# S5 recurrence of context and latents as one run of 80 states on VectorE

## The chip, the cores and the metric

The kernel runs on one core of a Trainium2 chip. The metric is the device time of one execution in microseconds (us). The engines are TensorE (PE in the profile), VectorE (DVE), ScalarE (ACT), GpSimd (POOL) and SyncE (SP, which here only starts DMAs). Each runs its own instructions in the order in which the program lists them for it, and waits on semaphores for the others.

## The reference, cut to what matters

One inference step through two trunk layers on 640 tokens: 128 of a context (a prompt) and 512 latents. Each layer projects the normed tokens to four mixers that run beside each other (a bidirectional state space model, SSD; a bidirectional S5; differential attention; windowed attention), gates and sums them, and ends with an MLP. The change is in S5, a linear recurrence with complex, diagonal coefficients over tokens, forward and backward, for 32 groups of 16 channels with 64 states each:

```python
def s5_direction(u, lam_re, lam_im, log_step, b_re, b_im, c_re, c_im, s0_re, s0_im):
    step = jnp.exp(log_step.astype(f32))[:, None]
    mag = jnp.exp(lam_re * step)
    ab_re = mag * jnp.cos(lam_im * step)
    ab_im = mag * jnp.sin(lam_im * step)
...
    x_re = (coef_re * bu_re - coef_im * bu_im).at[:, 0].add(ab_re * s0_re - ab_im * s0_im)
    x_im = (coef_re * bu_im + coef_im * bu_re).at[:, 0].add(ab_re * s0_im + ab_im * s0_re)
...
    _, _, s_re, s_im = lax.associative_scan(combine, (a_re, a_im, x_re, x_im), axis=1)
    y = (jnp.einsum('blgn,gmn->blgm', s_re, c_re.astype(f32))
         - jnp.einsum('blgn,gmn->blgm', s_im, c_im.astype(f32)))
    return y, s_re[:, -1], s_im[:, -1]
```

The context starts from zero and its last state is an output. The latents start from a state that is an input (`state_s5`). Everything is float32.

## The kernel before

**Layout.** Tokens lie along the free dimension, features on the 128 partitions. Weights come by DMA as 128x512 tiles (`wr`); ScalarE casts each to a high part (`wh`, L214), and `sub_lo` (L198) subtracts to a low part (`wl`), on VectorE or, for every third tile, on GpSimd. A product is then three matmuls (L225, L226, L227), mostly with 320 columns. TensorE therefore waits for VectorE whenever a `wl` of VectorE comes late.

**The S5 branch.** It takes eight tokens per step, so 640 tokens are 80 steps: 16 of the context and 64 of the latents. Partitions 0 to 63 carry the forward direction and 64 to 127 the backward one. A state column of the tile `st` holds 64 numbers per partition: real and imaginary part of 32 groups. (In the trace `st` and the tile with the inputs and powers are both called `B`.)

- `s5_in` (L725 to L756) multiplies the inputs by a matrix, four groups at a time (L745, into `mx`), and ScalarE copies the increments into `st` with three copies per round (L750 to L752, eight rounds). Column 0 is set to zero, columns 1 to 16 are the context's increments; column 17 is the latents' opening state, copied by GpSimd (L755), and 18 to 81 are the latents' increments.
- `s5_scan` (L758 to L793) turns increments into states. One step `advance` (L760) adds the product of a state and a power of the coefficient to the next: two multiplications into a tile `sc` (L764, L765) and two additions into `st` (L767). The 80 steps are cut into ten blocks of eight. In seven levels all blocks advance by one step at once; then eight single steps, one behind the other, carry the last state of a block over to the next block's (64 elements each); then seven more levels add to the inner columns of each block its opening state times powers 1 to 7. The blocks are shared out: of the eight latent blocks VectorE has two and three (`SCAN = 5`, L54, as two separate parts of 128 and 192 elements), and GpSimd three (192 elements); GpSimd also has the two of the context (`ctx="p"`, L49).
- `s5_out` (L795 to L822) brings the states into the order of the groups with three ScalarE copies per round (`sn`, L807 to L809, eight rounds) and TensorE multiplies them by the output matrices (L814 to L816, into `pb`), 81 columns each.

**Order of the work.** The branches are generators, and the strings of `PLAN` (L58) say which generator makes its next step (`i` for s5_in, `s` for s5_scan, `o` for s5_out, `p` for the projection of the differential attention, `a` for its core, `x` for the projection of the SSD branch, `c` for its core, `g` for the gates, `v` for the window attention's keys). A scheduler then fixes the order of each engine's instructions by a simulated timeline, so an edit in one branch also reorders the others. What runs beside the scan in both layers: the norms and rotary factors of the attention's queries and keys (`qk_finish`, L1168: `qn` L1179, `qks` L1187, `qkn` and `qn` L1172 and L1190 on GpSimd), which TensorE transposes (L1204) and ScalarE evacuates (L1205); the scores and softmax of `diff_core` (`dm` L1426, `dp` L1449, transposes L1455); the convolution of the SSD branch, `cv` (L907, L911, L917: seven operations on 128x646 per tile, on VectorE), which TensorE transposes too; and the projections, with their `wh` and `wl`.

## Time and profile before

| | us |
|---|---|
| median of 3 runs | 3042.03 |
| lowest and highest run | 3039.22, 3045.7 |
| profiled execution, its own time | 3031.18 |
| its span in the trace | 3029.4 |

TensorE is busy 2841.5 us of the span, VectorE 1724.3, ScalarE 1180.8, GpSimd 970.2. The mean clock granted to TensorE is 0.972 of full speed. The first layer's scan begins 234 us after the span's start, the second layer's at 1701 us. In the rows further down, a time stamp counts from the start of the span. Each row of a timeline has the start, the duration, the engine, the line of the code, the operation, the tiles (output, then inputs) with their sizes, and in brackets how long the engine was idle before it and what it then waited for. Consecutive instructions of VectorE overlap in the records by some 0.07 us; where an engine goes on without a pause the distance from one start to the next is what an instruction takes of it.

### The profile page before, as it was taken

What the parts mean: (1) busy time and instruction counts of PE and PEld (TensorE: products, weight loads), DVE (VectorE), ACT (ScalarE), POOL (GpSimd) and SP (SyncE); (2) the same over time, 40 slices, a digit from 0 to 9 for tenths busy, and PEclk for the clock granted to TensorE, in tenths of its full rate; (3) what the DMA queues carried; (4) which work ended last, traced back from release to release, by engine and by line L of the source; (5) the groups of instructions that cost most, each with busy time, mean ns of one, the idle gap of its engine ahead of it and who ended that gap; (6) DMA issues with size and microseconds to landing.
All of it is one profiled execution on the core that took longest, in us unless ns stands there. A gap on an engine that the chain in (4) does not pass through costs nothing.

```text
span 3029.4 us, 54102 instructions
## 1 busy us (share of the span) xinstructions
PE 2841.5 (94%) x20782; PEld 2663.8 (88%) x20782; DVE 1724.3 (57%) x3730; ACT 1180.8 (39%) x2660; POOL 970.2 (32%) x1057
## 2 busy tenths in 40 slices
PE   7888898999899999999999889999999999999999
PEld 5888788898689888899998879888898999999999
DVE  7859847765643456646235686475666436433333
ACT  4343463343344242323234536523535434322322
POOL 3737506523212222424111670264131122211111
PEclk9989999999899999999999999999999999999999
DMA  6752253224432735434444323431252323222222
GB/s 238 239 180 90 71 152 111 81 90 134 145 109 72 239 102 174 146 115 154 153 146 132 121 82 111 140 107 58 91 181 86 110 87 112 63 77 74 74 77 84
DMA packets 241858, 364.21 MB, mean 120 GB/s; under 512 B 42272, under 2 KB 104480, under 8 KB 241600
## 3 DMA queue, kind: packets, MB, share of 16 engines
q1 hardware_dynamic: 226848, 336.97, 35.5%
q10 hardware_dynamic: 14752, 23.78, 2.1%
q8 instruction: 164, 2.69, 0.4%
q14 instruction: 94, 0.77, 0.1%
HBM read 294.98 MB, written 65.68 MB: 119 GB/s over the span
## 4 chain that ended last, share of the span: by engine, by line
PE 71%; DVE 15%; issue 4%; DMA 3%; ACT 3%; POOL 2%; SPq 0%; ACTq 0%; DVEq 0%; POOLq 0%
PE dn L225 20%; PE dn L226 19%; PE dn L227 19%; DVE wl L198 2%; DVE B L767 2%; PE mx L290 1%; PE mx L1287 1%; PE pb L1331 1%; PE mx L1461 1%; PE mx L1325 1%; PE mx L1416 1%; DMA sseg<-acum 1%; DVE sc L764 1%; DVE sc L765 1%; PE mx L745 1%
## 5 line engine op out<-in xcount | busy, mean ns | idle before, releaser
L198 POOL TENSOR_TENSOR wl<-wr,wh 128x512 fp32r<-128x512 f32 x207 | 282.6, 1366 | 1271.2 <-ACT wh L214 1151.3
L214 ACT CAST wh<-wr 128x512 fp32r<-128x512 f32 (+1 forms) x614 | 377.4, 620 | 612.9 <-PE dn L226 539.6
L198 DVE TENSOR_TENSOR wl<-wr,wh 128x512 fp32r<-128x512 f32 (+1 forms) x407 | 325.7, 804 | 304.7 <-ACT wh L214 297.3
L225 PE MATMUL dn<-hh,wh 128*128 128x320 f32 x1328 | 422.6, 319 | 8.4 <-ACT us L697 2.7
L227 PE MATMUL dn<-hh,wl 128*128 128x320 f32 x1328 | 420.2, 317 | 3.4 <-DVE wl L198 3.4
L226 PE MATMUL dn<-hl,wh 128*128 128x320 f32 x1328 | 420.1, 316 | 2.8 <-DVE hl L403 1.5
L225 PE MATMUL dn<-nh,wh 128*128 128x320 f32 x992 | 311.7, 315 | 6.6 <-DVE r L1755 6.6
L225 PE MATMUL dn<-fh,wh 128*128 128x320 f32 x1008 | 313.6, 311 | 2.0 <-DVE s5u L595 1.3
L226 PE MATMUL dn<-nl,wh 128*128 128x320 f32 x992 | 308.9, 312 | 3.9 <-DVE nl L403 1.6
L227 PE MATMUL dn<-fh,wl 128*128 128x320 f32 x1008 | 312.0, 310 | 0.0
L226 PE MATMUL dn<-fl,wh 128*128 128x320 f32 x1008 | 311.8, 309 | 0.0
L227 PE MATMUL dn<-nh,wl 128*128 128x320 f32 x992 | 308.0, 311 | 0.0
L226 PE MATMUL dn<-wl,hh 128*128 128x256 f32 (+1 forms) x880 | 258.2, 294 | 16.3 <-DVE wl L198 14.2
L225 PEld LDWEIGHTS dn<-hh,wh 128*128 128x128 f32 x1328 | 254.3, 192 | 16.5 <-issue 3.1
L225 PE MATMUL dn<-wh,hh 128*128 128x256 f32 (+1 forms) x880 | 259.7, 297 | 8.5 <-DVE dtraw L1216 4.2
L227 PEld LDWEIGHTS dn<-hh,wl 128*128 128x128 f32 x1328 | 254.2, 191 | 8.9 <-DVE wl L198 4.6
L226 PEld LDWEIGHTS dn<-hl,wh 128*128 128x128 f32 x1328 | 254.2, 191 | 7.1 <-POOL hl L198 2.1
L227 PE MATMUL dn<-wh,hl 128*128 128x256 f32 (+1 forms) x880 | 257.1, 293 | 0.0
L1547 DVE SCALAR_TENSOR_TENSOR x<-dn,mod,x 128x192 f32<-128x192 f32 (+2 forms) x240 | 98.0, 437 | 225.2 <-PE dn L227 222.2
L225 PE MATMUL dn<-B,wh 128*128 128x320 f32 x640 | 207.8, 326 | 15.1 <-ACT B L834 4.4
L226 PE MATMUL dn<-B,wh 128*128 128x320 f32 x640 | 203.4, 318 | 0.0
L227 PE MATMUL dn<-B,wl 128*128 128x320 f32 x640 | 201.3, 315 | 0.0
(400 smaller groups left out, 6715.0 us busy)
## 6 DMA issues: line engine op xcount, KB each, us to landing
wr<-in_w_fc_dram SPq DMA_DIRECT2D x256, 256.0 KB, 2.8
wa<-in_w_mod_dram SPq DMA_DIRECT2D x160, 256.0 KB, 4.5
wr<-in_w_gate_dram SPq DMA_DIRECT2D x128, 256.0 KB, 2.8
wr<-in_w_tok_dram SPq DMA_DIRECT2D x80, 256.0 KB, 2.9
wr<-in_w_branch_dram SPq DMA_DIRECT2D x64, 256.0 KB, 3.0
acc<-gth SPq DMA_DIRECT2D x48, 320.0 KB, 3.0
gold<-acc SPq DMA_DIRECT2D x48, 320.0 KB, 3.3
gate<-gah ACTq DMA_DIRECT2D x70, 160.0 KB, 2.0
```

The costliest lines, as they stand in the source:

```text
L198: engine.tensor_tensor(out=out, in0=full, in1=hi, op=ALU.subtract)
L214: nc.scalar.copy(out=hi, in_=raw)
L225: nc.tensor.matmul(ps, sh, vh, start=first, stop=False)
L226: nc.tensor.matmul(ps, sh, vl, start=False, stop=False)
L227: nc.tensor.matmul(ps, sl, vh, start=False, stop=last)
L290: nc.tensor.matmul(acc[r0:r0 + 32, i * 256:i * 256 + 256], cpad[:, k, :], raw(part, k // 2)[:, c0:c0 + 256], start=(n_ < 4), stop=(n_ >= 4),)
L745: nc.tensor.matmul(xs[:, ri, g * NI:(g + 1) * NI], pm[:, ri, g * 128:(g + 1) * 128], U[:, g0 + g], start=True, stop=True)
L764: ve.tensor_tensor(out=pair[:, 0], in0=src, in1=re.to_broadcast(shp), op=ALU.mult)
L765: ve.tensor_tensor(out=pair[:, 1], in0=src[:, :, ::-1], in1=im.to_broadcast(shp), op=ALU.mult)
L767: ve.tensor_tensor(out=dst, in0=dst, in1=pair[:, i], op=ALU.add)
L1287: nc.tensor.matmul(sc[:, n, c0:c0 + (k1 - k0) * 128], qT[rows[n], g, ct], kT[rows[n], k0:k1].rearrange("p k c -> p (k c)"), start=True, st ...
L1547: nc.vector.scalar_tensor_tensor(out=xs, in0=ps[:, c0:c1], scalar=mods[l][:, part * 8 + f, s:s + 1], in1=xs, op0=ALU.mult, op1=ALU.add)
```

## The change

The 16 context steps and the 64 latent steps become one run of 80 columns behind a zero column (`st` columns 0 to 80, no separate opening column), and all of it goes to VectorE.

- `s5_in` copies forward increments of context and latents apart, so that a round has four copies in place of three (the copy of 64x648 elements becomes one of 64x128 and one of 64x512); `s5_out` likewise. GpSimd's copy of the opening state (L755) goes.
- Seven levels: each does two multiplications of 128x640 and two additions, for all ten blocks at once (28 instructions in a layer).
- In place of single steps and inner levels: for each block from the second on, its opening state, broadcast, times powers 1 to 8 at once, so that all eight columns of the block come out together, two multiplications and two additions of 128x512 (nine blocks, 36 instructions). The block's last column is the next one's opening state, so the nine blocks follow one another.
- After the first of these, column 16 is the context's final state. VectorE copies it out (128x64, `s5fin`) for the output's DMA and writes the latents' opening state over it.
- Before there were, in a layer, 144 such instructions on VectorE (56 of 128 elements, 56 of 192 and 32 of 64) and 116 on GpSimd (56 of 192, 28 of 128, 32 of 64). The number of steps of the generator stays 15, and `PLAN` is unchanged.

```diff
--- before.py
+++ after.py
@@ -48,10 +48,8 @@
 
 ENG = dict(
     sub0="v", sub1="p", mf="p", ef="v", xd="p", xw="p", xD="p", off="p", z="v", qkn="p", qka="p", qkc="v",
-    merge="p", diff="v", ctx="p", mn="v",
+    merge="p", diff="v", mn="v",
 )
-
-SCAN = 5
 
 LOW = 3
 WM = 14
@@ -747,50 +745,42 @@
                     )
             xv = xs[:, :, :4 * NI].rearrange("p r (g i) -> p r g i", i=NI)
             sv = st.rearrange("p j r g -> p r g j")[:, :, g0:g0 + 4]
-            nc.scalar.copy(out=sv[0:64, :, :, 1:82], in_=xv[0:64])
+
+            nc.scalar.copy(out=sv[0:64, :, :, 1:17], in_=xv[0:64, :, :, 0:16])
+            nc.scalar.copy(out=sv[0:64, :, :, 17:81], in_=xv[0:64, :, :, 17:81])
             nc.scalar.copy(out=sv[64:128, :, :, 16:0:-1], in_=xv[64:128, :, :, 0:16])
-            nc.scalar.copy(out=sv[64:128, :, :, 81:17:-1], in_=xv[64:128, :, :, 17:81])
+            nc.scalar.copy(out=sv[64:128, :, :, 80:16:-1], in_=xv[64:128, :, :, 17:81])
             if b < 7:
                 yield
-        nc.gpsimd.tensor_copy(out=st[:, 17], in_=s0)
-        var["U"], var["st"], var["pw"] = U, st, pw
-
-    def s5_scan(l, st, pw):
-
-        def advance(ve, dst, src, re, im, n):
+        var["U"], var["st"], var["pw"], var["s0"] = U, st, pw, s0
+
+    def s5_scan(l, st, pw, s0):
+
+        nb = (NI - 1) // 8
+
+        def advance(dst, src, re, im, n):
 
             shp = (128, n, 2, 32)
-            pair = tw([128, 2, n, 2, 32], "sc")
-            ve.tensor_tensor(out=pair[:, 0], in0=src, in1=re.to_broadcast(shp), op=ALU.mult)
-            ve.tensor_tensor(out=pair[:, 1], in0=src[:, :, ::-1], in1=im.to_broadcast(shp), op=ALU.mult)
-            for i in range(2):
-                ve.tensor_tensor(out=dst, in0=dst, in1=pair[:, i], op=ALU.add)
-
-        def power(k):
-            return pw[:, k - 1, 0].unsqueeze(1).unsqueeze(1), pw[:, k - 1, 1:3].unsqueeze(1)
-
-
-        parts = [(nc.vector, 17, SCAN // 2), (nc.vector, 17 + SCAN // 2 * 8, SCAN - SCAN // 2)]
-        parts += [(nc.gpsimd, 17 + SCAN * 8, 8 - SCAN)] * (SCAN < 8) + [(eng("ctx"), 0, 2)]
+            for v, x in ((src, re), (src[:, :, ::-1], im)):
+                t = tw([128, n, 2, 32], "sc")
+                nc.vector.tensor_tensor(out=t, in0=v.to_broadcast(shp), in1=x.to_broadcast(shp), op=ALU.mult)
+                nc.vector.tensor_tensor(out=dst, in0=dst, in1=t, op=ALU.add)
+
         for k in range(1, 8):
-            for ve, j, n in parts:
-                e = j + 8 * n
-                advance(ve, st[:, j + 1 + k:e + 1:8], st[:, j + k:e:8], *power(1), n)
+            advance(
+                st[:, 1 + k:8 * nb + 1:8], st[:, k:8 * nb:8], pw[:, 0:1, 0:1], pw[:, 0:1, 1:3], nb
+            )
             yield
-        for b in range(8):
-            j = 17 + 8 * b
-            advance(nc.vector, st[:, j + 8:j + 9], st[:, j:j + 1], *power(8), 1)
-        advance(eng("ctx"), st[:, 16:17], st[:, 8:9], *power(8), 1)
-        yield
-        for k in range(1, 8):
-            for ve, j, n in parts:
-                e = j + 8 * n
-                if j == 0:
-                    advance(ve, st[:, 8 + k:9 + k], st[:, 8:9], *power(k), 1)
-                else:
-                    advance(ve, st[:, j + k:e:8], st[:, j:e:8], *power(k), n)
-            yield
-        sp.dma_start(out=o["state_s5"][l], in_=st[:, 16])
+        for b in range(1, nb):
+            advance(st[:, 8 * b + 1:8 * b + 9], st[:, 8 * b:8 * b + 1], pw[:, :, 0:1], pw[:, :, 1:3], 8)
+            if b == 1:
+
+                fin = tmp([128, 2, 32], "s5fin", bufs=1)
+                nc.vector.tensor_copy(out=fin, in_=st[:, 16])
+                nc.vector.tensor_copy(out=st[:, 16], in_=s0)
+                sp.dma_start(out=o["state_s5"][l], in_=fin)
+            else:
+                yield
 
     def s5_out(l, U, st, y_d):
 
@@ -804,9 +794,10 @@
             sp.dma_start(out=qm, in_=q_d[b])
             sn = tw([128, 2, 4, NI], "sn")
             sv = st.rearrange("p j r g -> p r g j")[:, :, g0:g0 + 4]
-            nc.scalar.copy(out=sn[0:64], in_=sv[0:64, :, :, 0:81])
+            nc.scalar.copy(out=sn[0:64, :, :, 0:17], in_=sv[0:64, :, :, 0:17])
+            nc.scalar.copy(out=sn[0:64, :, :, 17:81], in_=sv[0:64, :, :, 16:80])
             nc.scalar.copy(out=sn[64:128, :, :, 0:16], in_=sv[64:128, :, :, 15::-1])
-            nc.scalar.copy(out=sn[64:128, :, :, 16:81], in_=sv[64:128, :, :, 81:16:-1])
+            nc.scalar.copy(out=sn[64:128, :, :, 16:81], in_=sv[64:128, :, :, 80:15:-1])
             ys = pb1()
             for g in range(4):
                 dst = ys[:, g * NI:(g + 1) * NI]
@@ -1656,7 +1647,7 @@
                 u=lambda: s5_project(l, h, u_d),
                 v=lambda: wkv_project(l, h, g, var),
                 i=lambda: s5_in(l, u_d, var),
-                s=lambda: s5_scan(l, var["st"], var["pw"]),
+                s=lambda: s5_scan(l, var["st"], var["pw"], var["s0"]),
                 p=lambda: diff_project(l, 0, h, g, var),
                 a=lambda: diff_core(l, 0, var["qkv", 0], nlam, dss),
                 x=lambda: ssd_project(l, h, sr),
```

Where the orders differ, they do so from about the scan's neighbourhood of either layer to some hundred microseconds behind it.

VectorE at the start of the first layer's scan, before (`B_2351` is the tile of states, `B_2346` that of inputs and powers):

```order
L764 TENSOR_TENSOR sc_2469<-B_2351,B_2346 128x128
L765 TENSOR_TENSOR sc_2469<-B_2351,B_2346 128x128
L764 TENSOR_TENSOR sc_2474<-B_2351,B_2346 128x192
L765 TENSOR_TENSOR sc_2474<-B_2351,B_2346 128x192
L767 TENSOR_TENSOR B_2351<-B_2351,sc_2469 128x2x64
L767 TENSOR_TENSOR B_2351<-B_2351,sc_2474 128x3x64
L767 TENSOR_TENSOR B_2351<-B_2351,sc_2469 128x2x64
L767 TENSOR_TENSOR B_2351<-B_2351,sc_2474 128x3x64
L764 TENSOR_TENSOR sc_2489<-B_2351,B_2346 128x128
L765 TENSOR_TENSOR sc_2489<-B_2351,B_2346 128x128
```

and with the change (`qkn` and `qn` are tiles of the attention's norms, `qks` their rotary part):

```order
L766 TENSOR_TENSOR sc_2476<-B_2351,B_2346 128x640
L766 TENSOR_TENSOR sc_2479<-B_2351,B_2346 128x640
L1170 TENSOR_TENSOR qn_2953<-qkn_2954,rgain_766 128x256
L767 TENSOR_TENSOR B_2351<-B_2351,sc_2476 128x10x64
L1172 TENSOR_TENSOR qn_2980<-qkn_2981,rtab_2924 128x256
L1178 TENSOR_TENSOR qks_2984<-qkn_2981,rtab_2924 128x4x32 x2
L1172 TENSOR_TENSOR qn_2992<-qkn_2993,rtab_2924 128x256
L767 TENSOR_TENSOR B_2351<-B_2351,sc_2479 128x10x64
L1178 TENSOR_TENSOR qks_2996<-qkn_2993,rtab_2924 128x4x32 x2
L766 TENSOR_TENSOR sc_2482<-B_2351,B_2346 128x640
L766 TENSOR_TENSOR sc_2485<-B_2351,B_2346 128x640
L1172 TENSOR_TENSOR qn_3004<-qkn_3005,rtab_2924 128x256
```

Before, the two VectorE parts of a level stood together, eight short instructions in a row. Now a level is four long ones, and the products of the attention's norms stand between them.

VectorE in the second layer, the last two blocks with the change (`rs`, `rb`, `ry` are small steps of a reciprocal root, `wl` a low part of a weight tile that TensorE takes):

```order
L766 TENSOR_TENSOR sc_20162<-B_18430,B_18425 128x512
L182 TENSOR_TENSOR rs_19651<-ry_19649 128x10
L767 TENSOR_TENSOR B_18430<-B_18430,sc_20159 128x512
L184 SCALAR_TENSOR_TENSOR rb_19653<-rs_19651,rv_19639 128x10
L767 TENSOR_TENSOR B_18430<-B_18430,sc_20162 128x512
L186 SCALAR_TENSOR_TENSOR ry_19655<-rb_19653,ry_19649 128x10
L766 TENSOR_TENSOR sc_20264<-B_18430,B_18425 128x512
L766 TENSOR_TENSOR sc_20267<-B_18430,B_18425 128x512
L182 TENSOR_TENSOR rs_19657<-ry_19655 128x10
L196 TENSOR_TENSOR wl_20095<-wr_20092,wh_20094 128x512
```

A `wl` that comes in here has two multiplications of 512 elements and the rest of a block ahead of it.

TensorE around the first output matmul of S5 in the second layer, before (`cv` is the convolution's output, `pb` that of S5):

```order
L225 MATMUL dn_20634<-hh_17940,wh_20603 128x320
L226 MATMUL dn_20634<-hl_17941,wh_20603 128x320
L227 MATMUL dn_20634<-hh_17940,wl_20604 128x320
L815 MATMUL pb_20708<-sn_20704,qm_20702 128x81
L816 MATMUL pb_20708<-sn_20704,qm_20702 128x81
L814 MATMUL pb_20708<-B_18636,tm_20700 128x81
```

and with the change:

```order
L223 MATMUL dn_20104<-hh_17729,wh_20100 128x320
L224 MATMUL dn_20104<-hl_17730,wh_20100 128x320
L225 MATMUL dn_20104<-hh_17729,wl_20101 128x320
L806 MATMUL pb_20279<-sn_20274,qm_20272 128x81
L807 MATMUL pb_20279<-sn_20274,qm_20272 128x81
L805 MATMUL pb_20279<-B_18425,tm_20270 128x81
L223 MATMUL dn_20130<-hh_17729,wh_20094 128x320
L224 MATMUL dn_20130<-hl_17730,wh_20094 128x320
```

There are 76 matmuls of 128x320 less ahead of the first S5 matmul than before; they now stand behind it. In the first layer the difference is 20 of 128x320 more ahead of it, and ten transposes less.

## Rows read from the trace of the kernel before

**Rows 1.** The page, busy time of each engine.

```profile
PE 2841.5 (94%) x20782; PEld 2663.8 (88%) x20782; DVE 1724.3 (57%) x3730; ACT 1180.8 (39%) x2660; POOL 970.2 (32%) x1057
```

**Rows 2.** The chain of waits, stretch 180 to 340 us, shares by line.

```profile
by line: DVE B L767 12.8%; DVE cv L911 8.9%; DVE sc L764 7.2%; PE mx L745 7.0%; DVE sc L765 6.2%; DVE wl L198 5.9%; PE dn L225 5.7%; PE dn L226 5.6%; PE dn L227 5.6%; issue 5.3%; DMA B<-u_d 2.8%; DMA wr<-in_w_xbc_dram 2.6%; DMA gate<-gah 2.
```

**Rows 3.** Windows: length; busy PE, PEld, DVE, ACT, POOL (instructions); clock; DMA share, GB/s.

```profile
234.00:348.00 114.00, 89.98 (x588) 84.84 (x587) 108.20 (x221) 34.56 (x89) 95.51 (x145) 0.91 0.22 72
1701.00:1814.00 113.00, 89.89 (x616) 85.51 (x617) 105.56 (x254) 37.88 (x104) 93.79 (x153) 0.91 0.23 72
```

**Rows 4.** Windows of tile sc alone, the scan's own instructions: DVE, POOL.

```profile
225.00:365.00 140.00, 61.79 (x144) 74.46 (x116) 0.93 0.26 82
1695.00:1830.00 135.00, 61.93 (x144) 68.16 (x116) 0.91 0.26 81
```

**Rows 5.** VectorE's timeline, first layer.

```profile
234.33 0.70 DVE L765 TENSOR_TENSOR sc<-B,B 128x128 f32<-128x128 f32 x1
234.95 0.75 DVE L764 TENSOR_TENSOR sc<-B,B 128x192 f32<-128x192 f32 x1
...
243.90 0.28 DVE L765 TENSOR_TENSOR sc<-B,B 128x128 f32<-128x128 f32 x1
244.10 0.34 DVE L764 TENSOR_TENSOR sc<-B,B 128x192 f32<-128x192 f32 x1
244.37 0.34 DVE L765 TENSOR_TENSOR sc<-B,B 128x192 f32<-128x192 f32 x1
...
296.00 0.68 DVE L198 TENSOR_TENSOR wl<-wr,wh 128x512 fp32r<-128x512 f32 x1
296.61 0.21 DVE L767 TENSOR_TENSOR B<-B,sc 128x64 f32<-128x64 f32 x1
...
297.27 0.21 DVE L764 TENSOR_TENSOR sc<-B,B 128x64 f32<-128x64 f32 x1
...
372.21 0.88 DVE L911 SCALAR_TENSOR_TENSOR cv<-xp,cw,cv 128x646 f32<-128x646 f32 x1
373.01 0.88 DVE L1449 SCALAR_TENSOR_TENSOR dp<-dp,drc,dp 128x640 f32<-128x640 f32 x1
373.81 0.88 DVE L911 SCALAR_TENSOR_TENSOR cv<-xp,cw,cv 128x646 f32<-128x646 f32 x1
```

**Rows 6.** TensorE's timeline, first layer.

```profile
228.14 1.91 PE L745 MATMUL mx<-B,pm 128*128 128x81 f32 x16
242.62 0.59 PE L1204 MATMUL pa<-ident,qn 128*128 128x128 f32 x2 [4.45 <-DVE qn L1179]
...
252.68 0.31 PE L226 MATMUL dn<-hl,wh 128*128 128x320 f32 x1
252.83 0.31 PE L227 MATMUL dn<-hh,wl 128*128 128x320 f32 x1
...
344.76 1.12 PE L1204 MATMUL pa<-ident,cv 128*128 128x128 f32 x4 [10.58 <-DVE cv L917]
...
353.35 0.45 PE L815 MATMUL pb<-sn,qm 128*128 128x81 f32 x2 [0.65 <-ACT sn L808]
```

**Rows 7.** What TensorE waited for, 180 to 420 us: total, times, longest.

```profile
PE pa L1204 <- DVE cv L917: 16.6, 2, 10.6
```

**Rows 8.** The same for 1690 to 1830 us, second layer.

```profile
PE dn L226 <- DVE wl L198: 6.3, 2, 5.2
```

**Rows 9.** VectorE's timeline, second layer: the scan's first instruction.

```profile
1701.38 0.29 DVE L764 TENSOR_TENSOR sc<-B,B 128x128 f32<-128x128 f32 x1 [3.19 <-ACT B L752]
```

**Rows 10.** ScalarE's timeline, second layer: the copies behind the scan.

```profile
1812.73 1.14 ACT L809 COPY sn<-B 64x520 f32<-64x520 f32 x1 [2.30 <-POOL B L767]
1813.88 1.35 ACT L807 COPY sn<-B 64x648 f32<-64x648 f32 x1
1815.25 0.42 ACT L808 COPY sn<-B 64x128 f32<-64x128 f32 x1
```

**Rows 11.** L815 in the second layer, TensorE's first S5 output matmul.

```profile
L815 PE MATMUL pb<-sn,qm x8: 234/275/275, 1815.8 to 1823.4; 128*128 128x81 f32 x8
```

## The prediction

> **What bounds the kernel now.** The page comes first: TensorE is busy for 94% of the span, VectorE for 57%, GpSimd for 32% [rows 1]. A microsecond that VectorE saves counts only where TensorE waits for it or runs at a lower clock because of it. So the second view is the chain of waits in the stretch around the first scan: the largest shares are VectorE's (additions of the scan L767 12.8%, convolution 8.9%, multiplications 7.2% and 6.2%, `wl` 5.9%), ahead of TensorE's own lines [rows 2]. Third, the windows of the two scans: in 114 us and 113 us TensorE is busy 90 us each, VectorE 108.2 and 105.6, GpSimd 95.5 and 93.8, at a granted clock of 0.91 against 0.972 over the whole span [rows 3]. At full clock TensorE's work of the window is 90 x 0.91 = 82 us, so 32 us of the one and 31 us of the other are lost to waits and clock. That bounds what a faster VectorE can bring there. Fourth, the waits themselves: TensorE stands still 10.58 us for the convolution [rows 6, 7], 4.45 us for `qn` [rows 6], 5.2 us for a `wl` in the second layer [rows 8], each a product that VectorE makes between pieces of the scan. The scan's own result is needed at 353.35 in the first layer, where TensorE waits 0.65 us for `sn` [rows 6], and at 1815.8 in the second [rows 11], where the copy ahead of it had waited for GpSimd's last addition [rows 10].
>
> The sum is made against the profiled execution, 3031.18 us; the median of the runs is 10.85 us (0.36%) above it, and I take the gain of the one off the other.
>
> **Price of the recurrence.** VectorE's instructions overlap by 0.07 us, so I count from start to start. With GpSimd quiet, 192 elements take 0.27 (244.10 to 244.37), 128 take 0.20 (243.90 to 244.10), and 64 take 0.14 (0.21 less the overlap) [rows 5]. That makes 56 x 0.27 + 56 x 0.20 + 32 x 0.14 = 30.8 us per layer; measured are 61.8 and 61.9 [rows 4]. The other half is GpSimd's presence: at 234.33, with GpSimd at its own part, the 128 elements took 0.62 [rows 5].
>
> The trace has no product of 640 elements on VectorE. The step from 64 to 128 and from 128 to 192 is 0.065 to 0.07, so 512 come to 0.60 and 640 to 0.73. The nearest rows agree: a `wl` of 512 took 0.61 (296.00 to 296.61), operations with a scalar took 0.80 for 646 and 0.80 for 640 (372.21 to 373.01 to 373.81) [rows 5]. Lower end 0.73, upper end 0.80; I take 0.73, since a `wl` is the same kind of operation and lies on the line. After: 28 x 0.73 + 36 x 0.60 + 0.3 for the two short copies = 42.3 us per layer. At the upper end it is 2 us more.
>
> The Trainium skill gives another price: VectorE: DVE Perf Modes, The TRN2 errata, puts a float32 `tensor_tensor` at (N + 151)/0.96 ns, 691 ns for 512 and 824 ns for 640. By that the layer's recurrence would cost an estimated 48 us and the gain would fall by some 11 us over both layers. The `wl` row with 0.61 goes against it.
>
> **First layer.** Undisturbed, the companions in VectorE's order of that stretch (21 convolution steps and 4 `dp` at 0.80, 13 `wl` at 0.61, some 30 short ones) come to about 36 us by the same rows; with the recurrence 66.8. The window has 108.2 busy: 41.4 us is inflation, against 95.5 us of GpSimd, 0.43 us for each. GpSimd keeps 95.5 - 74.5 = 21 us [rows 3, 4], so 9 us of inflation stay. VectorE's idle time in the window was 114 - 108.2 = 6 us; I keep it. After: 42.3 + 36 + 9 + 6 = 93 us, from 234.1 to 327.5; with 3 us for the ScalarE copies and the first matmul, 331 in place of 353.3. The order has 20 matmuls of 128x320 (0.15 each, 252.68 to 252.83 [rows 6]) more and ten transposes less ahead of that point, 2.4 us of work. The gain is 22.5 + 2.4 = **25 us**.
>
> **Second layer.** The order pulls the first output matmul ahead of 76 matmuls of 128x320, and VectorE's last block ahead of part of the convolution: by the same prices only 19 us of companions stand before the scan's end. 42.3 + 19 + 7 (GpSimd's remainder, (93.8 - 68.2) x 73/113 = 16.5 us at 0.43 [rows 3, 4]) + 5 idle = 73 us, from 1701.4 [rows 9] to 1774.5, with 3 us for the copies 1777.5. The 76 matmuls (11.4 us) and 2.5 us of pushed-back convolution are still to be done: it is as if 1791.5 stood in place of 1815.8 [rows 11], **24 us**. Both are under the 32 and 31 us that the windows allow.
>
> **Edits taken at nothing or nearly.** ScalarE gets 16 more copies per layer: 648 elements took 1.35, 128 took 0.42, 520 took 1.14 [rows 10], so a split costs some 0.2 us each, 3 us of an engine that is busy 35 of 114 us [rows 3]; only the last rounds lie on the path, within the 3 us above. Were that cover gone, 3 us per layer. The same queue casts `wh`: a copy of `sn` that waits for the last block holds the next casts, as the one at 1812.73 did for 2.30 us [rows 10]. GpSimd's copy of the opening state goes, off the path. SP's queue keeps its number of DMAs; the state's output is issued early and nothing waits for it.
>
> **New waits, the deduction.** The scan's instructions grow from at most 0.34 to 0.6 and 0.73 us, in one queue that also makes what TensorE takes. In the new order 5 to 10 of VectorE's products per layer (`wl`, `qn`, the first `dp`) stand less than 3 us ahead of their use, behind one or two such instructions. With 15 of them at some 0.5 us, 7 us are lost. Lower bound 0 (they land on waits that exist), upper bound 20 (each behind a whole level of 2.9 us, half of them felt). **Sum:** 25 + 24 - 7 = 42 us, so the profiled execution goes to 2989 and the median to 3000.
>
> **Rivals.**
> 1. *Part of it, 8 to 25 us gained: about 3025.* Once VectorE is quick enough, the next late thing sets the pace: `wl` behind its cast on ScalarE, the DMA of weights, or the convolution, whose products still follow in the same queue (16.6 us of waits in two places [rows 7]). For it: before the change TensorE waited for several sources, and one that goes uncovers another. Against it: VectorE's time for the first layer's stretch falls from 114 to 93 us, and the sum has already kept its idle time.
> 2. *Hidden, no change: 3042.* TensorE has 94% of the span; the waits could come again elsewhere in full, since the output of the S5 branch is only one of four that the gates need. Against it: the 32 and 31 us lost lie within the scans, at VectorE's own products. No measurement of this kernel can tell less than 0.2%, 6 us, from no change.
> 3. *Slower: 3063.* The moved work makes VectorE the one queue for everything. If the inflation stays though GpSimd leaves (because it comes from VectorE's own reads or from the DMAs, not from GpSimd), the factor is 108.2/66.8 = 1.62, and the first layer's 42.3 + 36 = 78 us become 127, 13 us more than the window's 114, and the second layer's some 8 us more, because its order ends sooner: 21 in all. It decides from a factor of 114/78 = 1.46 on, or 1.38 with the idle time. For it: the scan has more elements on VectorE than before (36,352 against 19,968 per partition). Against it: the quiet stretch at 243.90, where the same instructions took 0.20 instead of 0.62 [rows 5]. The Trainium skill, Perfetto Trace Analysis, Optimizing Scalar/DVE Operations, advises to offload from a saturated VectorE, even to GpSimd, and to break instructions up where they cause bubbles elsewhere; this change does the opposite on both counts. The page adds that GpSimd and VectorE share a read port, so that offloading may not help; the rows agree with that part.
>
> That the change does not do what it says can be left out: in the order all 64 scan instructions of a layer stand on VectorE, and none on GpSimd.
>
> **How the numbers follow.** The forecast with its own range of 2980 to 3017 (a gain of 62, all that the windows allow, to one of 25) has a chance of 0.63; rival 1 0.20, rival 2 0.08, rival 3 0.09. All of the forecast and most of rival 1 are faster by over 0.2%, so 0.82; within it 0.09; slower 0.09. For 8 in 10 the range leaves out the slower case and some of the upper tail of the gain: 2976 to 3034.
>
> **What would show it.** In the changed profile: multiplications of 128x640 at about 0.8 us (0.73 from start to start) and those of 512 at 0.67; VectorE's `sc` and `B` of the scan at 42 to 50 us per layer; GpSimd at about 828 us (970.2 less the 142.6 of its share); the first output matmul of S5 near 330 in the first layer and 20 to 40 us earlier in the second; the wait for the convolution smaller than 10 us; the clock in the windows over 0.93. Wrong: 640 elements at 1 us or more though GpSimd is quiet; `wl` of VectorE as the largest wait of TensorE; or a span that gets the gain back behind the scan, with TensorE waiting for the casts.

## The result and the profile after

The changed kernel takes 2995.37 us (median of 4 runs, 2991.5 to 2997.65) against 3040.62 us before (4 runs, 3038.88 to 3045.7): a ratio of 0.9847, with a 95% interval of 0.983 to 0.9864, or 41 to 52 us. The forecast was 3000, a gain of 42; the medians gained 45.3. Its profiled execution has a span of 2992.4 us, 37.0 less than the one before; that one took 3031.18 us, 0.31% under the 3040.62, so the two profiles show less than the medians. In the comparisons further down the kernel before came to 3035.3 to 3039.2 us.

The page's first part, after, beside [rows 1]. VectorE is busy 38.0 us less, GpSimd 137.4 less (forecast: 142.6), TensorE 9.7 less although it does the same work: less of it at the lower clock.

```profile
PE 2831.8 (95%) x20782; PEld 2651.5 (89%) x20782; DVE 1686.3 (56%) x3574; ACT 1181.3 (39%) x2692; POOL 832.8 (28%) x823
```

The window of the first scan, with the columns of [rows 3]: TensorE is busy 106.7 of 114 us where it was 90, and the granted clock is 1.00 where it was 0.91. VectorE is nearly as busy as before, but ahead with its work.

```profile
234.00:348.00 114.00, 106.70 (x748) 101.87 (x747) 104.89 (x163) 50.60 (x121) 29.65 (x35) 1.00 0.29 92
```

The scan's own instructions in either layer (busy time of VectorE and their number), beside [rows 4]: 46.8 and 49.2 us, where VectorE had 61.8 and 61.9 and GpSimd 74.5 and 68.2 beside it.

```profile
225.00:365.00 140.00, 46.79 (x64) 1.00 0.33 105
1660.00:1830.00 170.00, 49.15 (x64) 0.97 0.36 110
```

VectorE's timeline in the first layer, beside [rows 5]. Two multiplications of 640 take 1.47 from start to start (248.84 to 250.31), 0.735 each, an addition 0.74; two of 512 take 1.21, 0.605 each. The last instruction of the scan starts at 324.07.

```profile
248.84 1.55 DVE L766 TENSOR_TENSOR sc<-B,B 128x640 f32<-128x640 f32 x2
250.31 0.81 DVE L767 TENSOR_TENSOR B<-B,sc 128x640 f32<-128x640 f32 x1
251.05 0.15 DVE L1435 RECIPROCAL drc<-dsm 128x2 f32<-128x2 f32 x1
...
300.33 1.28 DVE L766 TENSOR_TENSOR sc<-B,B 128x512 f32<-128x512 f32 x2
301.54 0.20 DVE L1437 SCALAR_TENSOR_TENSOR drc<-drc,dnl,dsm 128x1 f32<-128x1 f32 x1
...
324.07 0.69 DVE L767 TENSOR_TENSOR B<-B,sc 128x512 f32<-128x512 f32 x1
```

TensorE's first output matmul of S5 in either layer, beside [rows 6, 11]: 329.9 and 1768.9, where it was at 353.35 and 1815.8. Of the second layer's 46.9 us, 13.7 were there when its scan began (1687.66, where it was 1701.38), so the layer itself gave 33, within the 20 to 40 that were named as a sign.

```profile
L806 PE MATMUL pb<-sn,qm x64: 231/275/275, 329.9 to 412.4; 128*128 128x81 f32 x64
L806 PE MATMUL pb<-sn,qm x64: 231/275/338, 1768.9 to 1903.7; 128*128 128x81 f32 x64
```

What TensorE waited for from 180 to 420 us, beside [rows 7]: the convolution is gone from the list, and of VectorE's products the costliest is a `wl` with 1.1 us.

```profile
PE pa L1195 <- ACT dq L1196: 2.6, 1, 2.6
PE dn L223 <- ACT gah L1480: 1.6, 1, 1.6
PE pa L1195 <- ACT d L1196: 1.6, 1, 1.6
PE mx L743 <- DMA B<-u_d: 1.4, 1, 1.4
PE pa L1195 <- POOL qn L1181: 1.3, 1, 1.3
PE dn L223 <- ACT xp L893: 1.3, 1, 1.3
PE dn L225 <- DVE wl L196: 1.1, 1, 1.1
...
PE pa L1195 <- DVE qn L1170: 0.7, 2, 0.4
```

**Where the time came from.** Two events divide each layer: the last of S5's input matmuls (the start of the stretch that holds the scan) and the first matmul of the SSD core's segment sums (`sseg`); the next is the first matmul of the window attention. Columns as in [rows 3]. Before:

```profile
229.80:480.20 250.40, 213.62 (x1477) 201.32 (x1476) 182.61 (x355) 116.70 (x249) 114.98 (x165) 0.95 0.35 105
480.20:779.00 298.80, 283.30 (x2024) 262.47 (x2024) 192.26 (x408) 113.07 (x290) 127.34 (x120) 0.95 0.36 112
1697.40:1964.80 267.40, 235.45 (x1671) 224.29 (x1670) 191.45 (x392) 129.91 (x287) 116.40 (x183) 0.95 0.35 105
1964.80:2268.90 304.10, 286.52 (x2041) 268.09 (x2041) 204.93 (x419) 115.55 (x295) 127.94 (x121) 0.95 0.36 109
```

After:

```profile
230.90:464.20 233.30, 215.68 (x1526) 203.74 (x1525) 161.57 (x282) 121.89 (x265) 47.11 (x49) 0.99 0.39 116
464.20:762.90 298.70, 278.66 (x1978) 257.18 (x1978) 191.49 (x404) 109.07 (x283) 128.49 (x120) 0.94 0.36 110
1683.80:1929.70 245.90, 233.66 (x1699) 222.88 (x1698) 173.91 (x315) 130.12 (x295) 49.51 (x65) 0.98 0.39 116
1929.70:2231.90 302.20, 281.12 (x2016) 261.46 (x2014) 207.54 (x418) 115.41 (x296) 128.35 (x122) 0.96 0.35 109
```

The scan's stretch falls from 250.4 to 233.3 us in the first layer and from 267.4 to 245.9 in the second. The stretch behind, from the SSD core to the window attention, stays: 298.8 to 298.7, and 304.1 to 302.2. Together 17.1 + 0.1 + 21.5 + 1.9 = 40.6; all other stretches of the program are 3.6 us longer in the profiled execution, and 37.0 remain.

### The profile page after: what moved, and what is told of

Same layout as the page of the kernel before. It is cut to its first block, busy times and chain, and to the rows that moved or that the text cites. A ratio compares the mean times of both kernels' runs of the same rounds, so it can differ in the third digit from the quotient of the medians.

```text
span 2992.4 us, 53739 instructions
## 1 busy us (share of the span) xinstructions
PE 2831.8 (95%) x20782; PEld 2651.5 (89%) x20782; DVE 1686.3 (56%) x3574; ACT 1181.3 (39%) x2692; POOL 832.8 (28%) x823
## 4 chain that ended last, share of the span: by engine, by line
PE 72%; DVE 13%; DMA 4%; issue 3%; ACT 2%; POOL 2%; SPq 0%; DVEq 0%; ACTq 0%; POOLq 0%
PE dn L223 20%; PE dn L224 20%; PE dn L225 20%; DVE wl L196 2%; DMA sseg<-acum 1%; PE mx L288 1%; PE mx L1278 1%; PE pb L1322 1%; PE mx L1407 1%; PE mx L1452 1%; PE mx L1316 1%; DVE B L767 1%; DVE sc L766 1%; PE mx L743 1%; DVE cv L902 1%
## 5 line engine op out<-in xcount | busy, mean ns | idle before, releaser
L224 PE MATMUL dn<-wl,hh 128*128 128x256 f32 (+1 forms) x880 | 256.8, 293 | 10.5 <-DVE wl L196 8.5
```

Source lines behind the costliest of these rows:

```text
L224: nc.tensor.matmul(ps, sh, vl, start=False, stop=False)
```

## The experiments

Three questions were put: is it GpSimd's presence that slowed VectorE, is it enough to move the work, and does the order that comes with the change matter. Times are medians; the kernel before had 3036.28 us beside e1 to e4, 3035.27 beside e5 to e8 and 3039.16 beside e9 to e12. It had 3040.62 beside the changed kernel, so a distance to the changed kernel (2995.37) crosses rounds; taken through the kernel before of each round, those of e2, e3 and e5 to e9 come out 1 to 6 us larger.

**e1: the old form, all on VectorE**

```diff
-    merge="p", diff="v", ctx="p", mn="v",
+    merge="p", diff="v", ctx="v", mn="v",
...
-SCAN = 5
+SCAN = 8
```

> The old form of the recurrence (levels, single steps, powers; 82 columns), but all ten blocks on VectorE. Theory A (the gain is GpSimd's contention that goes): VectorE's recurrence is now 112 instructions of 256 elements (about 0.34 each), 28 of 128, 64 of 64: about 53 us per layer, less than the 61.8 of before though it has all the work, and the companions lose their inflation; the time falls by 20 to 32 us against before, and the 11 us per layer of VectorE time between 53 and 42 are what the compact form adds to the gain. Rival B (the gain is the compact form, fewer and longer instructions, or the new order that comes with it): the old form on one engine has more instructions in one queue and stays within 6 us of before or gets slower.

Measured: 3035.5 us, ratio to before 1.0002 (0.9987 to 1.0016). No gain at all: theory A in this form fell. The scan's instructions on VectorE (columns as above):

```profile
225.00:420.00 195.00, 59.87 (x204) 0.97 0.37 114
1640.00:1860.00 220.00, 61.67 (x204) 0.94 0.39 124
```

I had put 53 us from start to start; they are busy 59.9 and 61.7 us (some 55 and 58 from start to start), as much as VectorE's smaller share took before. Moving the work alone is an exchange: the inflation goes and GpSimd's share comes. But the stretches say that this is not all of it:

```profile
230.10:487.30 257.20, 232.22 (x1610) 219.48 (x1608) 180.48 (x430) 126.78 (x265) 53.52 (x54) 0.96 0.37 111
487.30:782.10 294.80, 269.32 (x1892) 249.53 (x1892) 181.72 (x395) 104.82 (x274) 121.44 (x116) 0.94 0.34 107
1704.60:1972.00 267.40, 246.63 (x1778) 234.61 (x1778) 186.09 (x458) 134.57 (x301) 61.69 (x67) 0.96 0.35 108
1972.00:2273.70 301.70, 277.44 (x1934) 257.79 (x1934) 201.86 (x412) 109.97 (x282) 128.42 (x120) 0.92 0.34 107
```

In the first layer TensorE did 232.2 us of work in the scan's stretch, 18.6 more than before, and had less to do in the one behind (269.3 against 283.3), which took 294.8 us, only 4.0 less. Most of what was brought forward was not given back.

**e2: five products of GpSimd beside every step of the changed kernel**

```diff
+            du = tmp([128, 384], "s5du", bufs=1)
+            nc.gpsimd.tensor_copy(out=du[:, 0:1], in_=dst[:, 0, 0, 0:1])
+            for _ in range(5):
+                nc.gpsimd.tensor_tensor(out=du[:, 0:192], in0=pwf[:, 0:192], in1=pwf[:, 192:384], op=ALU.mult)
```

These lines stand in `advance`, behind the additions of each step; `pwf` is the tile of powers.

> The changed kernel, and beside every step of its recurrence five products of 128x192 from SBUF on GpSimd into a scratch tile that nobody reads (80 per layer, some 60 to 70 us; VectorE's order in the first layer is that of the changed kernel). Theory A (contention): VectorE is slowed again by some 0.43 us for each microsecond of GpSimd, 25 to 30 us per layer; the first output matmul of S5 moves from 330 to 345 to 358, and the whole is 25 to 50 us slower than the changed kernel, so near the kernel before. Rival B (form or order): within 6 us of the changed kernel, since VectorE's instructions and their order are the same and GpSimd has time for it.

Measured: 3044.22 us, ratio to before 1.0025 (1.0011 to 1.0039), 49 us above the changed kernel. VectorE's scan instructions, the same as in the changed kernel, are busy 64.1 and 58.3 us:

```profile
225.00:420.00 195.00, 64.08 (x64) 0.96 0.31 100
1640.00:1860.00 220.00, 58.26 (x64) 0.91 0.34 110
```

VectorE's timeline: two multiplications of 640 that GpSimd's products do not meet take 1.54 in all (241.35), additions that they meet 1.23 and 1.22 instead of 0.81.

```profile
241.35 1.54 DVE L767 TENSOR_TENSOR sc<-B,B 128x640 f32<-128x640 f32 x2
245.91 1.23 DVE L768 TENSOR_TENSOR B<-B,sc 128x640 f32<-128x640 f32 x1
...
252.36 1.22 DVE L768 TENSOR_TENSOR B<-B,sc 128x640 f32<-128x640 f32 x1
```

GpSimd's timeline beside the last of these:

```profile
251.72 1.18 POOL L772 TENSOR_TENSOR s5du<-B 128x192 f32<-128x192 f32 x1
```

The first output matmul of S5 goes from 329.9 to 356.2. The first layer's scan stretch, with the same matmuls as in the changed kernel and every VectorE instruction of that layer in the same order, takes 258.2 us in place of 233.3:

```profile
231.20:489.40 258.20, 224.14 (x1525) 209.88 (x1525) 189.66 (x282) 122.88 (x266) 129.79 (x146) 0.95 0.34 105
```

Theory A stands, B falls: all of the gain, and a little more, is gone with no change of form. GpSimd is busy 166 us more (999.1 against 832.8), VectorE 52 us more for the same instructions: 0.31 us for each, where I had taken 0.43.

**e3: the same with memsets**

```diff
-            for _ in range(5):
-                nc.gpsimd.tensor_tensor(out=du[:, 0:192], in0=pwf[:, 0:192], in1=pwf[:, 192:384], op=ALU.mult)
+            for _ in range(12):
+                nc.gpsimd.memset(du, 0.0)
```

> As e2, but GpSimd makes 12 memsets of 128x384 beside every step (192 per layer, some 70 us) with no operand to read; the order of the other engines is nearly that of the changed kernel. If the contention is one of reads from SBUF: within 6 us of the changed kernel, and multiplications of 128x640 stay at 0.81 us. If any activity of GpSimd slows VectorE (a shared write path, or DMA descriptors): 20 to 50 us slower, as e2.

Measured: 2996.83 us, ratio 0.9871 (0.9843 to 0.9899): as the changed kernel. GpSimd is busy 175 us more (1007.8 against 832.8), as much as in e2, and VectorE only 5 us more; the first layer's scan stretch takes 235.9 us, with VectorE's order in that layer again that of the changed kernel. A GpSimd that is busy with memsets hardly slows VectorE; one that reads operands from SBUF does.

```profile
225.00:420.00 195.00, 49.41 (x64) 0.99 0.38 117
1640.00:1860.00 220.00, 50.56 (x64) 0.98 0.41 127
```

**e4: the split copies alone**

```diff
-            nc.scalar.copy(out=sv[0:64, :, :, 1:82], in_=xv[0:64])
+            nc.scalar.copy(out=sv[0:64, :, :, 1:18], in_=xv[0:64, :, :, 0:17])
+            nc.scalar.copy(out=sv[0:64, :, :, 18:82], in_=xv[0:64, :, :, 17:81])
...
-            nc.scalar.copy(out=sn[0:64], in_=sv[0:64, :, :, 0:81])
+            nc.scalar.copy(out=sn[0:64, :, :, 0:17], in_=sv[0:64, :, :, 0:17])
+            nc.scalar.copy(out=sn[0:64, :, :, 17:81], in_=sv[0:64, :, :, 17:81])
```

> The kernel before with the ScalarE copies of s5_in and s5_out split as in the change (four in place of three per round, 16 more per layer), the recurrence untouched. My sum put them at 0.2 us each, hidden but for the last round: 0 to 6 us slower than before. If they lie on the path, in ScalarE's queue ahead of the casts: more than 6 us slower, and the change would gain by avoiding them.

Measured: 3038.93 us, ratio 1.0005 (0.9991 to 1.0019). That is 2.7 us above the kernel before, within the 0 to 6 of the sum: hidden.

**e5 to e8: sizes, forms and doses**

e5 cuts each instruction of the changed recurrence in two:

```diff
-                nc.vector.tensor_tensor(out=t, in0=v.to_broadcast(shp), in1=x.to_broadcast(shp), op=ALU.mult)
-                nc.vector.tensor_tensor(out=dst, in0=dst, in1=t, op=ALU.add)
+                vb, xb = v.to_broadcast(shp), x.to_broadcast(shp)
+                for hn in (slice(0, n // 2), slice(n // 2, n)):
+                    nc.vector.tensor_tensor(out=t[:, hn], in0=vb[:, hn], in1=xb[:, hn], op=ALU.mult)
+                for hn in (slice(0, n // 2), slice(n // 2, n)):
+                    nc.vector.tensor_tensor(out=dst[:, hn], in0=dst[:, hn], in1=t[:, hn], op=ALU.add)
```

> The changed kernel with each of the 64 instructions of a layer's recurrence cut into two halves (five blocks or four powers each): 128 instructions, the same elements, 64 x 0.07 = 4.5 us more of VectorE per layer. Theory A (VectorE's undisturbed price sets the time): 3 to 9 us slower than the changed kernel. Theory C (long instructions in the one queue hold up what TensorE waits for): equal or up to 8 us faster. Theory D (what e1 lost was lost to the order that the scheduler made for it, not to VectorE's price): a change of anything between 0 and 35 us that goes with no price; the stretch from the last input matmul of S5 to the start of the SSD core then takes as much TensorE work and ends late, as in e1.

Measured: 3003.22 us, ratio 0.9892 (0.9874 to 0.991), 8 us above the changed kernel, 13 when taken through the kernel before. The long instructions hold up nothing that costs more than their saving; theory C falls. The 8 are not price alone, since the order moved too: the first layer's scan stretch has 1585 matmuls where the changed kernel has 1526.

e6 keeps the compact levels and layout, with the old second half:

```diff
-            advance(st[:, 8 * b + 1:8 * b + 9], st[:, 8 * b:8 * b + 1], pw[:, :, 0:1], pw[:, :, 1:3], 8)
+            advance(st[:, 8 * b + 8:8 * b + 9], st[:, 8 * b:8 * b + 1], pw[:, 7:8, 0:1], pw[:, 7:8, 1:3], 1)
...
+        for k in range(1, 8):
+            advance(
+                st[:, 8 + k:8 * nb:8], st[:, 8:8 * nb:8], pw[:, k - 1:k, 0:1], pw[:, k - 1:k, 1:3], nb - 1
+            )
+            yield
```

> The compact layout and the compact first seven levels; the second half in the old way (nine single steps of 64 elements, then seven levels over nine blocks, 576 elements). Price on VectorE by start-to-start rows: 28 x 0.735 + 36 x 0.14 + 28 x 0.67 = 44 us per layer against 42 of the changed kernel. Theory A: within 6 us of the changed kernel (2993 to 3005). Theory D: up to 35 us slower than it, since the order is another. A rival to both, that the single steps cannot be pipelined and each waits for the one before: 36 x some 0.2 us more, still under 8 us per layer.

Measured: 3019.16 us, ratio 0.995 (0.9932 to 0.9967), 24 us above the changed kernel, far more than the 2 us of price per layer; theory A falls here, and theory D's range holds it. VectorE's scan instructions are busy 52.0 and 53.3 us. The first layer's two stretches take 1.8 us more together than in the changed kernel; in the second the scan's stretch takes 12 us longer, with 10.5 us more of TensorE's work in it:

```profile
1688.30:1946.20 257.90, 244.20 (x1778) 232.75 (x1776) 177.84 (x346) 132.33 (x304) 55.50 (x65) 0.98 0.36 111
```

e7 is e1 with the eight latent blocks as one part:

```diff
-        parts = [(nc.vector, 17, SCAN // 2), (nc.vector, 17 + SCAN // 2 * 8, SCAN - SCAN // 2)]
+        parts = [(nc.vector, 17, SCAN)]
...
-            pair = tw([128, 2, n, 2, 32], "sc")
+            pair = [tw([128, n, 2, 32], "sc") for _ in range(2)]
```

> As e1 (old form, all on VectorE), but the eight latent blocks as one part in place of two, with two tiles sc in place of a pair: 56 instructions of 512 elements, 28 of 128 and 64 of 64, by start-to-start rows 48 us per layer, 5 less than e1 and 6 more than the changed kernel. Theory A (price): 8 to 15 us slower than the changed kernel, 25 to 35 us faster than before; then e1's 204 short instructions were its fault. Theory D (order): anywhere between the changed kernel and e1.

Measured: 3015.18 us, ratio 0.9942 (0.9925 to 0.9959): 20 us better than e1, 20 worse than the changed kernel. That is outside theory A's 8 to 15 us, and theory D allowed anything in between. VectorE's scan instructions are busy 56.5 and 58.5 us, 6.5 us in both layers together less than e1's 121.5.

In the second layer e1, e6, e7 and e11 (below) have the same number of matmuls in the scan's stretch, 1778, and so allow a comparison of the form at equal TensorE work. The stretch takes 257.9 us in e6, 260.8 in e7, 264.2 in e11 and 267.4 in e1, where the scan's instructions are busy 53.3, 58.5, 62.5 and 61.7: at equal TensorE work the form costs about its price. The rows of e7 and e11:

```profile
1689.90:1950.70 260.80, 245.29 (x1778) 234.35 (x1777) 181.97 (x402) 135.15 (x301) 55.42 (x68) 0.97 0.36 110
1725.00:1989.20 264.20, 245.61 (x1778) 234.16 (x1777) 184.86 (x457) 133.87 (x299) 57.06 (x67) 0.96 0.36 109
```

The changed kernel has 1699 matmuls there and 245.9 us. The step of 12 us to e6 goes with the 79 matmuls more (some 12 us at 0.15 each) that its order put ahead of the SSD core; the stretch behind has 80 fewer and still takes 304.6 us, 2.4 more.

e8 is e2 with `range(2)`:

> As e2 with two products of GpSimd per step in place of five, 32 per layer, some 25 to 28 us; the orders of the other engines are nearly those of the changed kernel. Theory A with contention in proportion: e2's 48 us for 80 products make some 19 us for 32, so 3010 to 3018. If TensorE has slack that hides a first dose: within 6 us of the changed kernel. If contention is all or nothing (the first products already push VectorE behind TensorE's need): 30 us or more.

Measured: 3017.4 us, ratio 0.9927 (0.9902 to 0.9952), 22 us above the changed kernel. GpSimd is busy 88.8 us more than in the changed kernel (921.6), so 0.25 us of time for each; in e2 it was 49/166 = 0.29. The cost goes with the dose. One of its six runs, 2997.33 us, is as fast as the changed kernel, while the others lie between 3013.9 and 3018.9; why is not known.

```profile
225.00:420.00 195.00, 56.38 (x64) 0.97 0.37 114
1640.00:1860.00 220.00, 54.41 (x64) 0.96 0.40 125
```

**e9 to e12: the plan**

In all ten kernels so far, the stretch from the SSD core to the window attention took 295 to 300 us in the first layer. So the start of the SSD core seemed to decide, and gate steps ahead of it to be in the way. e9 moves six gate steps of the first layer's plan:

```diff
-        "sisppppppiiippsisisasgssssappsssaxssgpsappxgxaaiagaaaagxcgaoogoccxcclooxscggcglgllccglPgogcgAPPA"
+        "sisppppppiiippsisisasgssssappsssaxsspsappxxaaiaaaaaxcaoooccxcclooxscggcglgllcggggggcglPgogcgAPPA"
```

> The changed kernel with one edit of the first layer's plan: six gate steps (g) that stood ahead of and among the first steps of the SSD core go behind its eighth step; by the order some 27 us of TensorE work less stands between S5's input matmuls and the first matmul of the SSD core (that on sseg), and as much more behind it. Over the ten kernels so far, the stretch from that matmul to the window attention's first took 295 to 299 us in the first layer, whatever TensorE work between 253 and 272 us at full clock lay in it. Theory D (when the SSD core begins decides, and the stretch behind is of fixed length): the SSD core begins 12 to 25 us earlier, the stretch behind stays under 305, and the whole is 8 to 20 us faster than the changed kernel. Rival E (the work is only moved, and the stretch behind grows by as much as it gets): within 6 us of the changed kernel.

> As e9 with seven gate steps in either layer (in the second some 5 us of TensorE work less ahead of the SSD core). Theory D: another 2 to 6 us faster than e9. Rival E: as the changed kernel.

> e1 (old form, all on VectorE) with e9's edit of the plan; by the order the first layer then has the same TensorE work ahead of the SSD core (143 us) and behind it (239 us) as e9. Theory D: what e1 lost in the first layer was the work that its order put ahead of the SSD core; now the SSD core begins 20 to 35 us earlier than in e1, and only the price of the old form on VectorE (53 against 42 us) remains, 5 to 12 us behind e9 at that point; the whole 15 to 30 us faster than e1. If e1 lost to its short instructions themselves: no more than 8 us faster than e1.

> The kernel before with e9's edit of the plan, so again the same 143 and 239 us of TensorE work in the first layer, with GpSimd's share of the recurrence still there. Theory A with D: VectorE, slowed by GpSimd, bounds this stretch; the SSD core begins 0 to 12 us earlier than in the kernel before and 20 to 35 us later than in e9, the whole 0 to 10 us faster than before. If TensorE's work ahead of the SSD core alone decides: as e9, 25 to 35 us faster than the kernel before in the first layer.

Measured: e9 3022.77 us (ratio 0.9947, 0.9927 to 0.9967), e10 3035.89 (1.0004, 0.999 to 1.0018), e11 3055.83 (1.0063, 1.0042 to 1.0084), e12 3064.34 (1.0091, 1.0071 to 1.0111). Theory D fell, and so did rival E: e9, e11 and e12 are 20 to 28 us slower than the same kernel with the old plan, and e10, with the second layer's gates too, 41. The first layer's two stretches, e9:

```profile
229.80:465.60 235.80, 206.40 (x1343) 192.47 (x1342) 160.27 (x282) 115.05 (x252) 40.10 (x47) 0.90 0.33 99
465.60:785.80 320.20, 304.97 (x2161) 285.00 (x2161) 190.55 (x404) 117.74 (x298) 132.00 (x123) 0.95 0.37 115
```

e11:

```profile
229.10:478.80 249.70, 211.32 (x1343) 195.25 (x1341) 168.53 (x420) 113.88 (x241) 50.59 (x48) 0.87 0.32 93
478.80:801.80 323.00, 304.39 (x2161) 284.32 (x2161) 192.26 (x404) 118.13 (x298) 131.68 (x123) 0.95 0.36 114
```

e12:

```profile
230.70:489.10 258.40, 213.98 (x1343) 198.36 (x1342) 179.66 (x360) 112.78 (x241) 113.35 (x163) 0.86 0.30 90
489.10:809.80 320.70, 304.14 (x2162) 283.67 (x2161) 190.86 (x404) 118.28 (x298) 131.30 (x123) 0.95 0.36 114
```

All three have the same TensorE work in the scan's stretch (1343 matmuls). In e9 it got 183 matmuls less than in the changed kernel and took 235.8 us, no less than the 233.3: TensorE idled, and ran at a clock of 0.90 on average. The stretch behind then did grow, to 320 us, now that it had more work than those 295 to 300 us hold.

But the edit did not only take gate steps away. It also let the scheduler reorder VectorE: between the scan's first and last instruction stand 42 operations of the convolution where the changed kernel has 24, and the scan ends at 339.1 us in place of 324.8. The SSD core did not begin 12 to 25 us earlier, as theory D's forecast had supposed (465.6 against 464.2), and TensorE waits for the convolution again (8.1 us). The operations on `cv` from the scan's first to its last instruction, the changed kernel and e9:

```profile
235.50:324.80 89.30, 21.15 (x24) 1.00 0.29 96
235.30:339.10 103.80, 38.06 (x42) 0.92 0.22 69
```

So e9 to e12 do not tell what less TensorE work alone would do.

Among themselves, these three are the best comparison of the form in the first layer: with equal TensorE work, and 216 to 218 other instructions of VectorE in each, the scan's stretch takes 258.4 us with GpSimd's share (e12), 249.7 with the old form on VectorE (e11) and 235.8 with the compact form (e9). Of 22.6 us, 8.7 come from moving the work off GpSimd and 13.9 from the form it takes on VectorE. In the whole program e11 is 8.5 us faster than e12.

## Why the prediction was right

- **What bounds the stretch: right for the first layer, in part for the second.** VectorE between the scan and its companions. The waits for its products (16.6 us for the convolution [rows 7]) went, the clock in the window rose from 0.91 to 1.00, and e2 brought the time back by slowing VectorE, with the same instructions in the same order in the first layer. That GpSimd's leaving would by itself be worth 20 to 32 us (e1's expectation) was wrong.
- **The price of the new instructions: right.** 0.73 and 0.60 forecast, 0.735 and 0.605 measured. By the formula quoted from the Trainium skill (VectorE: DVE Perf Modes, The TRN2 errata) 640 elements are 0.824 and 512 are 0.691; those fit what the trace records as the duration of one (0.81 and 0.68) but not what an instruction takes of the engine when another follows at once. The row decided, and rightly. One reason given with the rows was wrong: at 243.90 GpSimd was not quiet. It had an addition open there for 3.14 us, where the same operation takes 0.74 at 250.87, and it ended 0.6 us after VectorE paused at 246.40. As these records have it, VectorE, going on without a pause, held GpSimd out, and in turn stood idle 2.03 us for GpSimd's next product; the changed kernel has the same at 239.24 (3.45 us). The prices were undisturbed all the same, but the row is no case of a silent GpSimd, as the words against rival 3 take it to be:

```profile
243.85 3.14 POOL L1190 TENSOR_TENSOR qn<-qn,qks 128x256 f32<-128x256 f32 x1 [1.84 <-DVE qks L1187]
248.43 0.80 DVE L1181 TENSOR_TENSOR qn<-qkn,rtab 128x256 f32<-128x256 f32 x1 [2.03 <-POOL qkn L1172]
```

- **The first layer's scan: right.** 327.5 forecast for its end, some 324.8 measured; the first output matmul 331 forecast, 329.9 measured. Of the 93 us that were summed, 89.3 came, with VectorE busy 87.8 of them: its idle time fell from 6 us to 1.5, which the sum had kept. The gain of 25 us is there at that point: 23.4, with the forecast 2.4 of work ahead of it. At the SSD core 17.1 are left.
- **The second layer: right.** 73 us forecast from the scan's first instruction to its end; 71.6 measured (1687.7 to 1759.3, where ScalarE's copy starts behind the last addition). The gain in the two stretches is 23.4, against 24. One thing the account leaves out: in this layer of the kernel before, VectorE's last scan instruction began at 1800.50, while GpSimd's share ended near 1813, which is what the copy at 1812.73 waited for [rows 10]. So some 12 us of the scan's length there were GpSimd's own queue, and not VectorE slowed by it.

```profile
1759.34 1.12 ACT L798 COPY sn<-B 64x512 f32<-64x512 f32 x1 [0.41 <-DVE B L767]
```

The kernel before:

```profile
1800.50 0.35 DVE L767 TENSOR_TENSOR B<-B,sc 128x192 f32<-128x192 f32 x1
```

- **The deduction of 7 us: right in size by luck, wrong in its reason.** I had it for products of VectorE that come late behind long instructions. TensorE's waits for VectorE in the stretch are small (1.1 and 0.7 us in the list above), and halves (e5) make nothing better. What went instead is in the first layer's two stretches: TensorE did 215.7 x 0.99 = 213.5 us of work at full clock in the scan's stretch, where it was 213.6 x 0.95 = 202.9, with 49 matmuls more, and the stretch behind, with 46 matmuls less, took as long as before. Of the 25 us only 17.1 were left there; late products do not show in the 8 us. The other stretches lost 3.6 us more, so the profiled execution gained 37.0 where 42 were forecast. The median then came out 5 us below the forecast and not above it, because the sum carried over the 10.85 us by which the profile before lay under its median, and the changed kernel's profile lies only 1.2 us under its own; that is luck too.
- **Inflation: right in kind, too large.** I reckoned 0.43 us of VectorE for each of GpSimd, all inflation put down to it; e2 and e8 show 0.31 and 0.29 (25.7/88.8) of VectorE's time. What the rest is in the kernel before stays open: a price of the companions that was too low, or short instructions that lose more (128 elements went from 0.20 to 0.62 at 234.33 [rows 5], 640 elements from 0.74 to 1.15 in e2).
- **The rivals.** Rival 3, that the inflation stays though GpSimd leaves, did not come: 46.8 and 49.2 us. Rival 1 came in part: the first layer's 8 us are a gain that the next stretch did not pass on. The Trainium skill (Perfetto Trace Analysis, Optimizing Scalar/DVE Operations), named with rival 3, says that offloading a saturated VectorE, even to GpSimd, may make sense, and that breaking up instructions may help where an engine that is not saturated holds up others; here the offloaded form is the slower one at the same form and plan (e12 against e11, 8.5 us), and halves cost 8 us (e5). What the Trainium skill says there of a shared read port agrees with e2 and e3.

What I had not seen is how much the gain hangs on the form. I argued from GpSimd's leaving; e1 shows that this alone brings nothing as the scheduler then orders it, and 8.7 us in the first layer at equal TensorE work. Both are needed: with all of it on VectorE the compact form gains 40 us over the old one (e1 to the changed kernel), and in the compact form contention costs 49 (e2). The two do not add up to a loss of the kernel before, which has its contention but also only part of the elements on VectorE; e1 exchanges the one for the other.

**Open.** e6 and e1 are slower than VectorE's price tells (24 us over the changed kernel for some 5 us per layer, and 20 us over e7 for 3). The scan's length on VectorE tells more than the price of its instructions: in the first layer it takes 89.3 us from the first to the last one in the changed kernel, 98.1 in e7, 107.9 in e1 and 115.4 in e2, and the two stretches together take 532.0, 541.0, 552.0 and 557.7. The kernel before does not fall in line (113.7 and 549.2). In the second layer e6 and e1 have 79 matmuls more in the scan's stretch than the changed kernel. How much each order, that on VectorE and that on TensorE, costs was not told apart: e2, e3 and e8 hold VectorE's order in the first layer, but no run held it while the form changed. No version here beats the changed kernel.

## What to carry to other kernels

VectorE and GpSimd, both reading SBUF, were not two engines here: before sharing elementwise work with GpSimd, price what its reading does to VectorE's other products, in the stretch where VectorE is the bound. If the work comes back to VectorE, change its form as well: 64 instructions in place of e1's 204, over the same states, were worth more than the move. And read the gain behind the next stretch, not at the end of the work that became faster; and when a plan is edited, look at the order of every engine, since e9's edit of TensorE's work moved VectorE's.

## What the runs showed of the hardware

GpSimd slows VectorE by what it reads: 80 products from SBUF per layer cost VectorE 52 us in all for 166 us of GpSimd, 192 memsets per layer 5 us for 175 (e2, e3). It goes by dose (e8: 26 us for 89). It works the other way too: while VectorE went on without a pause, a GpSimd addition stayed open for 3.14 us, where the same takes 0.74 (kernel before, 243.85 and 250.87). And where TensorE idled between waits its granted clock was lower: 0.90, 0.87 and 0.86 of full clock over the scan's stretch (e9, e11, e12), against 0.99, 0.96 and 0.95 in the same three kernels with the old plan.
